# Linear attention on one core: K and V in 8 KB rows, V by DMA into zeroed blocks, the first matmul in 64x64 tiles

## The chip, the cores and the metric

The kernel runs on 1 core of one Trainium2 chip. The metric is device time of one execution, in microseconds. The time before is 126.32 us, the median of 3 runs (126.27 to 126.68).

## The reference

Inputs Q, K and V are float32 of shape (8, 12, 512, 64): 96 heads of 512 rows of 64 numbers. Each head is on its own.

```python
Q_feat = np.maximum(0, Q) + 1
K_feat = np.maximum(0, K) + 1
KV = np.einsum('bhkd,bhkv->bhdv', K_feat, V)
K_sum = np.sum(K_feat, axis=2)
numerator = np.einsum('bhqd,bhdv->bhqv', Q_feat, KV)
denominator = np.einsum('bhqd,bhd->bhq', Q_feat, K_sum)
return (numerator / (denominator[:, :, :, None] + 1e-10)).astype(np.float32)
```

So per head: a 64x64 matrix KV and a 64-vector K_sum from K and V, then for each row of Q a row of 64 numbers and its divisor. 12.6 MB come in three times, 12.6 MB go out.

## The kernel before, in words

Work goes in 12 groups of eight heads, and two groups make a round of sixteen heads (1 MB of bf16 for each of K, V and Q). All loads but the first half of Q are DMAs from POOL that cast float32 to bf16. SP loads that first half in float32 into an output buffer.

*Loads.* `load` (L115) brings K and V with 16 rows of a head in a partition: 4 KB read, 2 KB written in one run, 32 consecutive partitions to a head. `load_q` (L121) brings Q with 32 rows in a partition: 8 KB read, 4 KB written. After the first round, which is loaded in halves, a load of K, V or Q is one DMA of 128 partitions.

*First matmul.* `k_features` (L151, DVE) writes max(K + 1, 1) to a tile of its own. A partition holds rows of one head of four, so V must be spread out for the matmul: `v_blocks` (L167, L169) copies the 32 partitions of head b to columns 64b of `v_all`, zeros elsewhere (three copies on DVE, the fourth on ACT). `v_all` is zeroed once by `clear` (L254, L255), which also writes four columns of ones (L256). `keys_values` (L185) then does 16 x 2 matmuls per group, each with 128 rows of contraction, 64 columns of K and 260 of `v_all`: four heads' KV and their K_sum. The two of a pair go to the two halves of the columns of the array. ACT copies the results to `kva_all` (L195, L196), which is block-diagonal over two heads and cleared once by POOL (L276).

*Second matmul.* `q_features` (L151) and `transposes` (L206, with copies out of PSUM at L209, nearly all on ACT) bring Q into place. `out_matmuls` (L219) fills two PSUM tiles of two banks, `norms` does a reciprocal (L236) and a product (L237) for each of them on DVE and writes `o_sb`.

*Stores.* `store` puts the first ten of twelve groups out from POOL (L135), the last two from SP (L140 to L148), the last one in pieces. All stores are kept behind the loads in POOL's queue: four of them follow the last load, the others come one by one.

The order on every engine is the order of the program text (`tc.manual_schedule()`). A load waits until the tile's last reader is done (`IN_BUFS = 2`). `psum`, which the outputs use, has two tiles in all, so a chunk's matmuls wait for the norms of the chunk before it. DMAs from POOL use eight semaphores in turn, so one waits for the eighth before it to land.

Of the kernel before, what the change touches and what calls it, by code (L numbers as in the profile page):

```python
# [12 lines left out]
BANK = 512  # L13
IN_BUFS = 2
OUT_BUFS = 5
LAG = 3
# [3 lines left out]
def kernel(  # L20
# [15 lines left out]

# [5 lines left out]
    C2 = 2 * C  # L45
    C4 = 4 * C
    R = 4
    NPAIR = B * H * S // (P * C)
    NP = 4
    NG = NPAIR // NP  # L50
# [3 lines left out]
    def view(t, c):  # L54
        return t.flatten_outer_dims().rearrange("(n p c) d -> p n c d", p=P, c=c)

    q_eights = view(Q, C4)
    k_dram = view(K, C2)
    v_dram = view(V, C2)
    o_dram = view(out, C)  # L60
# [3 lines left out]
    kf_pool = ctx.enter_context(tc.tile_pool(name="kf_pool", bufs=2))  # L64
# [8 lines left out]
    identity = const.tile([P, P], BF16, name="identity")  # L73
    NV = 4
    v_all = const.tile([P, 2, 2, C2, 4 * D1], BF16, name="v_all")
    ones = const.tile([P, 4], BF16, name="ones")
    zero = const.tile([P, 1], FP32, name="zero")
    kva_all = const.tile([P, NV, 4, 2, D1], BF16, name="kva_all")
    kva_diag = [kva_all[:, i] for i in range(NV)]

    drams = dict(k=k_dram, v=v_dram)
    raw = {}
    bufs = {}
    kfs = {}
    qfs = {}
    qts = {}
    outs = {}
    cells_of = {}
# [7 lines left out]
    def load_rest_q(t):  # L96
        u = in_pool.tile([P, 2, C4, D], BF16, name="q_raw")
        nc.gpsimd.dma_start(out=u[:, 1], in_=q_eights[:, 1])
        for e in range(2):
            raw["q", e] = [  # L100
                x.rearrange("p (r c) d -> p r c d", c=C)[:, :, 4 * e : 4 * e + 4]
                for x in (t, u[:, 1])
            ]

    def load(x, groups):
        s = groups[0] // 2
        if groups[0] % 2 == 0 or (x, s) not in bufs:
            bufs[x, s] = in_pool.tile([P, 4, C2, D], BF16, name=f"{x}_raw")
        if len(groups) == 2:
            ms = slice(0, 4)  # L110
            of = slice(4 * s, 4 * s + 4)
        else:
            ms = slice(groups[0] % 2, 4, 2)
            of = slice(4 * s + groups[0] % 2, 4 * s + 4, 2)
        nc.gpsimd.dma_start(out=bufs[x, s][:, ms], in_=drams[x][:, of])  # L115
        for g in groups:
            raw[x, g] = bufs[x, s][:, g % 2 : 4 : 2]

    def load_q(s):
        t = in_pool.tile([P, 2, C4, D], BF16, name="q_raw")  # L120
        nc.gpsimd.dma_start(out=t, in_=q_eights[:, 2 * s : 2 * s + 2])  # L121
        rows = t.rearrange("p n (r c) d -> p n r c d", c=C)
        for e in range(2):
            raw["q", 2 * s + e] = [rows[:, n, :, 4 * e : 4 * e + 4] for n in range(2)]

    def load_pair(s):
        load("k", (2 * s, 2 * s + 1))
        load("v", (2 * s, 2 * s + 1))
        load_q(s)

    def store(g):
        s = g // 2
        o_to = o_dram[:, 2 * NP * s : 2 * NP * s + 2 * NP]
        if g < NG - 2:
            nc.gpsimd.dma_start(  # L135
                out=o_to[:, g % 2 : 2 * NP : 2], in_=outs[s][:, g % 2 : 2 * NP : 2], single_packet=True
            )
            return
        if g == NG - 2:
            nc.sync.dma_start(out=o_to[:, 0 : 2 * NP : 2], in_=outs[s][:, 0 : 2 * NP : 2])  # L140
            return
        o_sb = outs[s]
# [12 lines left out]
    def k_features(g):  # L155
        k_raw = raw.pop(("k", g))
        kf = kf_pool.tile([P, C2, 2, D], BF16, name="kf")
        for n in range(2):
            feature(kf[:, :, n], k_raw[:, n])
        kfs[g] = kf  # L160

    def v_blocks(g):
        v_raw = raw.pop(("v", g))
        for b in range(4):
            ps = slice(32 * b, 32 * b + 32)
            if b == 3:
                nc.scalar.copy(out=v_all[ps, g % 2, :, :, b * D : b * D + D], in_=v_raw[ps])  # L167
            else:
                nc.vector.tensor_copy(  # L169
                    out=v_all[ps, g % 2, :, :, b * D : b * D + D], in_=v_raw[ps]  # L170
                )

    def q_features(g):
        q_raw = raw.pop(("q", g))
        qf = qf_pool.tile([P, R, C // 2, 2, D], BF16, name="qf")
        for n in range(2):
            feature(qf[:, :, :, n], q_raw[n])
        qfs[g] = qf

    def keys_values(g):  # L180
        kf = kfs.pop(g)
        kva_ps = psum_kva.tile([P, 4 * D1], FP32, name="kva_ps")
        for c in range(C2):
            for n in range(2):
                nc.tensor.matmul(  # L185
                    kva_ps[64 * n : 64 * n + 64],
                    lhsT=kf[:, c, n, :],
                    rhs=v_all[:, g % 2, n, c, :],
                    start=(c == 0),
                    stop=(c == C2 - 1),  # L190
                )
        kva = kva_diag[g % NV]
        for n in range(2):
            ps = slice(64 * n, 64 * n + 64)
            nc.scalar.copy(out=kva[ps, :, n, 0:D], in_=kva_ps[ps, 0 : 4 * D].rearrange("p (b d) -> p b d", b=4))  # L195
            nc.scalar.copy(out=kva[ps, :, n, D], in_=kva_ps[ps, 4 * D : 4 * D1])  # L196

    def transposes(g):
        qf = qfs.pop(g)
        if g % 2 == 0:  # L200
            qts[g // 2] = mid_pool.tile([P, C, P, R], BF16, name="qt")
        for half in range(2):
            qt_ps = psum_qt.tile([P, 2, R, P], BF16, name="qt_ps")
            for c in range(2):
                for r in range(R):
                    nc.tensor.transpose(qt_ps[:, c, r], qf[:, r, 2 * half + c, :, :], identity)  # L206
            copy = nc.vector.tensor_copy if half and g == NG - 2 else nc.scalar.copy
            lo = g % 2 * 4 + 2 * half
            copy(out=qts[g // 2][:, lo : lo + 2], in_=qt_ps.rearrange("p c r q -> p c q r"))  # L209

    def out_matmuls(g, h):
        qt = qts[g // 2]
        kva = kva_diag[(g // 2 * 2 + h) % NV]
        ops = [psum.tile([P, 2, BANK], FP32, tag="ps", name="o_ps") for _ in range(2)]
        for c in range(C):
            for j in range(2):
                b = 2 * (g % 2) + j
                q = 16 * (4 * h + b)
# [3 lines left out]
                    rhs=kva[:, b],  # L222
# [3 lines left out]
        cells_of[g, h] = ops  # L226

    def norms(g, h):
        ops = cells_of.pop((g, h))
        if (g % 2, h) == (0, 0):  # L230
            outs[g // 2] = out_pool.tile([P, 2 * NP, C, D], FP32, name="o_sb")
        o_sb = outs[g // 2]
        for i in range(2):
# [4 lines left out]
                out=o_sb[:, 2 * h + g % 2 : 2 * NP : NP, 4 * i : 4 * i + 4].rearrange(  # L238
# [7 lines left out]
    def output(g):  # L246
        for h in range(2):
            out_matmuls(g, h)
            norms(g, h)

    def clear(i):
        t = v_all[:, i].rearrange("p n c x -> p (n c x)").bitcast(FP32)
        w = t.shape[1] * 5 // 8
        nc.vector.memset(t[:, 0:w], 0.0)  # L254
        nc.scalar.copy(out=t[:, w:], in_=zero.to_broadcast([P, t.shape[1] - w]))  # L255
        nc.vector.tensor_copy(  # L256
            out=v_all[:, i, :, :, 4 * D : 4 * D1].rearrange("p n c j -> p (n c) j"),
            in_=ones[:, None, :].to_broadcast([P, 2 * C2, 4]),
        )

    with tc.manual_schedule():
        nc.gpsimd.memset(zero, 0.0)
        q_first = load_first_q()
        load("k", (0,))
        load("v", (0,))
        load_rest_q(q_first)
        load("k", (1,))
        load("v", (1,))
        nc.vector.memset(ones, 0.0)
        for b in range(4):  # L270
            nc.vector.memset(ones[32 * b : 32 * b + 32, b : b + 1], 1.0)
        clear(0)
        make_identity(nc, identity)
        for t in kva_diag:
            for b in range(4):
                nc.gpsimd.memset(t[:, b], 0.0)  # L276
        load_pair(1)
        clear(1)
        last = NG - 1
        for g in range(last - 1):  # L280
            if g % 2:
                transposes(g - 1)
            k_features(g)
            v_blocks(g)
            if g >= 2:
                output(g - 2)
            if g % 2:
                transposes(g)
            else:
                q_features(g)  # L290
                q_features(g + 1)
            keys_values(g)
            if g % 2 and g // 2 + 2 < NG // 2:
                load_pair(g // 2 + 2)
            if g == NG - 5:
                for done in range(g - LAG):
                    store(done)
            if g >= NG - 5:
                store(g - LAG)
        k_features(last - 1)  # L300
        output(last - 3)
        out_matmuls(last - 2, 0)
        v_blocks(last - 1)
        k_features(last)
        v_blocks(last)
# [12 lines left out]
        for g in range(last - LAG, NG):  # L318
            store(g)
# [30 lines left out]
```

## Time and profile before

| | us |
|---|---|
| median of 3 runs | 126.32 |
| span of the profiled execution, first to last instruction | 124.5 |
| busy DVE | 89.7 |
| busy PE | 65.0 |
| busy ACT | 59.6 |
| busy POOL | 26.6 |

The page gives no other time of the profiled execution than its span; 1.8 us lie between the span and the median. Busy times are shares of the whole span and say nothing of who waits for whom. The rows "DMA" and "GB/s" cut the span in 40 slices of 3.1 us: 9 means that the 16 DMA engines were busy for 90% or more, and GB/s counts the bytes as written. "PEclk" is the clock granted to TensorE in tenths of full speed. A group's row has the busy time, the mean duration of one instruction, and the idle time before it with what ended it.

### The profile page before, as it was taken

How to read it: one execution, taken by the hardware profiler on the slowest of the kernel's cores; microseconds unless marked ns; L12 is line 12 of the kernel's file. 1: busy time of each engine (PE TensorE's matmuls, PEld its weight loads, DVE VectorE, ACT ScalarE, POOL GpSimd, SP SyncE). 2: the span in 40 equal slices, each digit the busy share in tenths (PEclk: the TensorE clock that was granted, in tenths of full speed). 3: DMA queues.
4: the chain of work that ended last, by engine and by line, in shares of the span. 5: the costliest groups of instructions: out<-in, count | busy, mean ns of one | idle time of the engine just before them, and what ended most of it. 6: DMA issues, size and time to landing. Idle time of an engine off the chain costs nothing.

```text
span 124.5 us, 2350 instructions
## 1 busy us (share of the span) xinstructions
PE 65.0 (52%) x960; PEld 53.1 (43%) x960; DVE 89.7 (72%) x190; ACT 59.6 (48%) x86; POOL 26.6 (21%) x53
## 2 busy tenths in 40 slices
PE   0000874600596837939197495987756987420000
PEld 0000754600475736829175374866635766210000
DVE  4875744206999989997999989999599996970000
ACT  7505069706009981398807767169990355000000
POOL 6992020400001310204002194202203302000000
PEclk9999999985559996799859959689985599955555
DMA  3999999999999999999999999999999999999993
GB/s 95 319 211 218 204 209 212 209 215 218 207 212 212 220 215 205 212 213 216 212 213 211 213 219 211 213 209 216 214 295 421 420 419 411 416 414 416 417 407 140
DMA packets 11971, 32.13 MB, mean 258 GB/s; under 512 B 568, under 2 KB 824, under 8 KB 11832
## 3 DMA queue, kind: packets, MB, share of 16 engines
q0 software_dynamic: 10592, 28.84, 97.5%
q1 hardware_dynamic: 1368, 3.15, 6.7%
q8 instruction: 7, 0.11, 0.3%
q14 instruction: 4, 0.03, 0.1%
HBM read 37.75 MB, written 12.58 MB: 404 GB/s over the span
## 4 chain that ended last, share of the span: by engine, by line
DMA 30%; DVE 27%; PE 14%; ACT 10%; POOL 6%; issue 3%; DVEq 0%; ACTq 0%; POOLq 0%
DMA v_raw<-in_V_dram 30%; DVE o_sb L237 12%; PE kva_ps L185 12%; DVE v_all L169 8%; ACT v_all L167 5%; ACT qt L209 3%; DVE recip L236 3%; DVE qf L151 2%; POOL kva_all L276 2%; POOL k_raw L115 2%; ACT kva_all L195 2%; PE qt_ps L206 1%; PE o_ps L219 1%; DVE kf L151 1%; POOL v_raw L115 1%
## 5 line engine op out<-in xcount | busy, mean ns | idle before, releaser
L185 PE MATMUL kva_ps<-v_all,kf 128*64 128x260 bf16 x384 | 34.2, 351 | 15.8 <-DVE v_all L169 14.2
L185 PEld LDWEIGHTS <-kf 128*64 128x64 bf16 x384 | 27.8, 144 | 19.7 <-DVE v_all L169 14.7
L237 DVE TENSOR_TENSOR o_sb<-o_ps,recip 128x512 f32<-128x512 f32 x48 | 33.2, 692 | 1.7
L219 PE MATMUL o_ps<-kva_all,qt 128*64 128x130 bf16 x384 | 19.6, 236 | 28.1 <-DVE recip L236 19.1
L169 DVE COPY v_all<-v_raw 32x2048 bf16<-32x2048 bf16 x36 | 25.5, 710 | 10.5 <-DMA v_raw<-in_V_dram 10.1
L219 PEld LDWEIGHTS <-qt 128*64 128x64 bf16 x384 | 13.7, 116 | 33.1 <-issue 16.9
L167 ACT COPY v_all<-v_raw 32x2048 bf16<-32x2048 bf16 x12 | 22.6, 1894 | 10.8 <-DMA v_raw<-in_V_dram 10.6
L195 ACT CAST kva_all<-kva_ps 64x256 bf16<-64x256 f32 x24 | 8.9, 370 | 31.4 <-PE kva_ps L185 31.2
L209 ACT COPY qt<-qt_ps 128x1024 bf16<-128x1024 bf16 x23 | 22.2, 1015 | 2.5 <-PE qt_ps L206 2.2
L206 PE MATMUL qt_ps<-identity,qf 128*128 128x128 bf16 x192 | 14.1, 229 | 1.3 <-ACT qt L209 1.1
L135 POOL DMA_DIRECT2D out_dram<-o_sb x10 | 8.8, 879 | 23.1 <-DMA q_raw<-in_Q_dram 6.7
L206 PEld LDWEIGHTS <-qf 128*128 128x128 bf16 x192 | 11.8, 103 | 4.1 <-issue 2.2
L115 POOL DMA_DIRECT2D k_raw<-in_K_dram x7 | 5.4, 772 | 37.5 <-DVE kf L151 37.0
L151 DVE TENSOR_SCALAR kf<-k_raw 128x1024 bf16<-128x1024 bf16 x24 | 9.9, 453 | 4.3 <-DMA k_raw<-in_K_dram 4.2
L236 DVE RECIPROCAL recip<-o_ps 128x8 f32<-128x8 f32 x48 | 9.6, 200 | 2.9 <-PE o_ps L219 2.6
L115 POOL DMA_DIRECT2D v_raw<-in_V_dram x7 | 5.4, 768 | 16.5 <-ACT v_all L167 16.5
L151 DVE TENSOR_SCALAR qf<-q_raw 128x1024 bf16<-128x1024 bf16 x22 | 8.1, 424 | 0.0
L254 DVE MEMSET v_all<- 128x2600 f32 x2 | 4.5, 2225 | 1.1 <-issue 1.1
L196 ACT CAST kva_all<-kva_ps 64x4 bf16<-64x4 f32 x24 | 4.1, 169 | 0.0
L121 POOL DMA_DIRECT2D q_raw<-in_Q_dram x5 | 3.5, 704 | 0.0
L255 ACT COPY v_all<-zero 128x1560 f32<-128x1560 f32 x2 | 2.9, 1488 | 0.0
L276 POOL MEMSET kva_all<- 128x130 bf16 x16 | 2.4, 196 | 0.0
(14 smaller groups left out, 6.6 us busy)
## 6 DMA issues: line engine op xcount, KB each, us to landing
out_dram<-o_sb POOLq DMA_DIRECT2D x10, 1024.0 KB, 24.0
k_raw<-in_K_dram POOLq DMA_DIRECT2D x5, 1024.0 KB, 16.7
v_raw<-in_V_dram POOLq DMA_DIRECT2D x5, 1024.0 KB, 17.3
q_raw<-in_Q_dram POOLq DMA_DIRECT2D x5, 1024.0 KB, 21.5
o_sb<-in_Q_dram SPq DMA_DIRECT2D x1, 1024.0 KB, 4.8
k_raw<-in_K_dram POOLq DMA_DIRECT2D x2, 512.0 KB, 9.5
v_raw<-in_V_dram POOLq DMA_DIRECT2D x2, 512.0 KB, 11.3
out_dram<-o_sb SPq DMA_DIRECT2D x1, 1024.0 KB, 12.1
```

The source lines that it names most:

```text
L115: nc.gpsimd.dma_start(out=bufs[x, s][:, ms], in_=drams[x][:, of])
L135: nc.gpsimd.dma_start(out=o_to[:, g % 2 : 2 * NP : 2], in_=outs[s][:, g % 2 : 2 * NP : 2], single_packet=True)
L151: nc.vector.tensor_scalar(out=dst, in0=src, scalar1=1.0, scalar2=1.0, op0=ALU.add, op1=ALU.max)
L167: nc.scalar.copy(out=v_all[ps, g % 2, :, :, b * D : b * D + D], in_=v_raw[ps])
L169: nc.vector.tensor_copy(out=v_all[ps, g % 2, :, :, b * D : b * D + D], in_=v_raw[ps])
L185: nc.tensor.matmul(kva_ps[64 * n : 64 * n + 64], lhsT=kf[:, c, n, :], rhs=v_all[:, g % 2, n, c, :], start=(c == 0), stop=(c == C2 - 1),)
L195: nc.scalar.copy(out=kva[ps, :, n, 0:D], in_=kva_ps[ps, 0 : 4 * D].rearrange("p (b d) -> p b d", b=4))
L206: nc.tensor.transpose(qt_ps[:, c, r], qf[:, r, 2 * half + c, :, :], identity)
L209: copy(out=qts[g // 2][:, lo : lo + 2], in_=qt_ps.rearrange("p c r q -> p c q r"))
L219: nc.tensor.matmul(ops[c // 4][64 * j : 64 * j + 64, c // 2 % 2, (c % 2) * W : (c % 2) * W + W], lhsT=qt[:, c, q : q + 16, :], rhs=kva[:, ...
L236: nc.vector.reciprocal(out=recip, in_=cells[:, :, :, :, D:D1])
L237: nc.vector.tensor_tensor(out=o_sb[:, 2 * h + g % 2 : 2 * NP : NP, 4 * i : 4 * i + 4].rearrange("p n (b c) d -> p b c n d", b=2), in0=cell ...
```

## The change

Sixteen heads are now one step, six in all. K and V are read with 32 rows of a head in a partition (8 KB read, 4 KB written), and heads are interleaved over the partitions: of each eight heads (the first eight are n = 0, the others n = 1), partition 4j + b holds rows of pair b, the first head of the pair in partitions 0 to 63 and the second in 64 to 127. Each load of K or V is four DMAs, one for each b, of 32 partitions with a step of 4.

V's DMAs write straight into `v_blocks`, nine blocks of 32 x 64 columns: block b for n = 0, b + 5 for n = 1, block 4 for the ones. It is zeroed once (`clear`) and never written elsewhere until the end, since partition 4j + b gets V in the blocks of b alone. The copies of V on DVE and ACT are gone. The ones come from a mask, a sum over the identity (`put_ones`).

K's features are written in place. `keys_values` does 32 x 4 matmuls per step, each with 64 rows of contraction (r), 64 columns of K (n) and 320 columns of `v_blocks`, to two PSUM tiles. It is cut in four parts, two of them ahead of the fourth chunk of outputs. `transposes` copies half of its results on DVE. The last two steps' outputs use the memory of `v_blocks` in place of an output buffer; there are four of those instead of five. The order of the main loop is new.

```diff
-OUT_BUFS = 5
-LAG = 3
+OUT_BUFS = 4
...
+    k_dram, v_dram = (
+        t.flatten_outer_dims().rearrange("(s n b j c) d -> s b j n c d", n=2, b=NB, j=J, c=C4)
+        for t in (K, V)
+    )
...
+    v_blocks = [const.tile([P, 2 * NB + 1, C4, D], BF16, name=f"v_blocks{i}") for i in range(2)]
...
+    def load_k(s):
+        k_raw[s] = in_pool.tile([P, 2, C4, D], BF16, name="k_raw")
+        for b in range(NB):
+            nc.gpsimd.dma_start(out=k_raw[s][b:P:NB], in_=k_dram[s, b])
+
+    def load_v(s):
+        for b in range(NB):
+            nc.gpsimd.dma_start(
+                out=v_blocks[s % 2][b:P:NB, b : b + NB + 2 : NB + 1], in_=v_dram[s, b]
+            )
...
-    def v_blocks(g):
-        v_raw = raw.pop(("v", g))
-        for b in range(4):
-            ps = slice(32 * b, 32 * b + 32)
-            if b == 3:
-                nc.scalar.copy(out=v_all[ps, g % 2, :, :, b * D : b * D + D], in_=v_raw[ps])
-            else:
-                nc.vector.tensor_copy(
-                    out=v_all[ps, g % 2, :, :, b * D : b * D + D], in_=v_raw[ps]
-                )
...
+    def k_features(s):
+        for n in range(2):
+            feature(k_raw[s][:, n], k_raw[s][:, n])
...
+    def keys_values(s, part):
+        if part == 0:
+            kva_ps[s] = [psum_kva.tile([P, BANK], FP32, name="kva_ps") for _ in range(2)]
+        kf = k_raw[s]
+        n_cols = (NB + 1) * D
+        for c in range(C4 // 4 * part, C4 // 4 * part + C4 // 4):
+            for n in range(2):
+                for r in range(2):
+                    ps = slice(64 * r, 64 * r + 64)
+                    nc.tensor.matmul(
+                        kva_ps[s][r][64 * n : 64 * n + 64, 0:n_cols],
+                        lhsT=kf[ps, n, c, :],
+                        rhs=v_blocks[s % 2][ps, NB * n : NB * n + NB + 1, c, :],
+                        start=(c == 0),
+                        stop=(c == C4 - 1),
+                    )
...
-            copy = nc.vector.tensor_copy if half and g == NG - 2 else nc.scalar.copy
+                copy = nc.vector.tensor_copy if half else nc.scalar.copy
...
+            if s < NS - 2:
+                outs[s] = out_pool.tile([P, 2 * NP, C, D], FP32, name="o_sb")
+            else:
+                t = v_blocks[s % 2].rearrange("p b c d -> p (b c d)").bitcast(FP32)
+                outs[s] = t[:, 0 : 2 * NP * C * D].rearrange("p (n c d) -> p n c d", n=2 * NP, c=C)
...
     def clear(i):
-        t = v_all[:, i].rearrange("p n c x -> p (n c x)").bitcast(FP32)
-        w = t.shape[1] * 5 // 8
+        t = v_blocks[i].rearrange("p b c d -> p (b c d)").bitcast(FP32)
+        w = t.shape[1] // 2
         nc.vector.memset(t[:, 0:w], 0.0)
         nc.scalar.copy(out=t[:, w:], in_=zero.to_broadcast([P, t.shape[1] - w]))
+
+    def put_ones(i):
         nc.vector.tensor_copy(
+            out=v_blocks[i][:, NB, :, 0:NB], in_=mask[:, None, :].to_broadcast([P, C4, NB])
         )
...
         q_first = load_first_q()
-        load("k", (0,))
-        load("v", (0,))
+        load_k(0)
         load_rest_q(q_first)
...
         clear(0)
+        load_v(0)
         make_identity(nc, identity)
...
+        load_k(1)
         clear(1)
...
+        load_v(1)
+        load_q(1)
...
+        for s in range(1, NS + 1):
+            if s + 1 < NS:
+                load_k(s + 1)
+                load_v(s + 1)
+                load_q(s + 1)
+            if s == NS - 2:
+                for g in range(2 * NS - 8):
+                    store(g)
+            if s < NS:
+                k_features(s)
+            for i in range(4):
+                out_matmuls(s - 1, *chunks[i])
+                if s < NS and i == 2:
+                    keys_values(s, 0)
+                    keys_values(s, 1)
+                norms(s - 1, *chunks[i])
+            if s < NS:
+                keys_values(s, 2)
+                keys_values(s, 3)
+                q_features(s)
+                keys_values_out(s)
+                transposes(s)
+            if s >= NS - 2:
+                for g in range(2 * s - 4, 2 * s - 2 if s < NS else 2 * NS):
+                    store(g)
```

## The prediction

> **What bounds the kernel now.** I read the page's slices first, then its queues, then the DMA issues.
>
> ```profile
> span 124.5 us, 2350 instructions
> ...
> DMA  3999999999999999999999999999999999999993
> GB/s 95 319 211 218 204 209 212 209 215 218 207 212 212 220 215 205 212 213 216 212 213 211 213 219 211 213 209 216 214 295 421 420 419 411 416 414 416 417 407 140
> ...
> q0 software_dynamic: 10592, 28.84, 97.5%
> q1 hardware_dynamic: 1368, 3.15, 6.7%
> q8 instruction: 7, 0.11, 0.3%
> ```
>
> The DMA row is full from the second slice to the last but one. Up to slice 30 the engines load at some 213 GB/s of bf16 written, which is 426 GB/s of float32 read; after that they store at 416 GB/s. So the span is one line of transfers: 37.75 MB in, 12.58 MB out, and what lies at its two ends. The chain of waits names DVE with 27%, but that chain runs beside a DMA that never rests, and POOL's long waits are for buffers, with transfers still queued:
>
> ```profile
> POOL k_raw L115 <- DVE kf L151: 37.0, 4, 14.0
> POOL v_raw L115 <- ACT v_all L167: 16.5, 4, 4.5
> ```
>
> The trace's records of single DMA packets give the rates (no view prints them). In them the first packet starts 1.8 us into the span and the last ends at 123.2. Each load ends with a tiny semaphore packet per engine. These lie 4.952 us apart for a whole load of K or V (32 packets per engine, 4 KB read each), 2.486 for a half (16 packets), 4.895 for a whole load of Q (16 packets, 8 KB read each) and 2.458 for a half (8 packets). Two equations each: a 4 KB packet takes 154.1 ns, an 8 KB one 304.6, and the end of a DMA 0.02 us (the semaphore packet itself is recorded with 22 ns).
>
> **The loads.** K and V go to 8 KB rows, Q's shape, but each load becomes four DMAs of 32 partitions. One quarter is 4 x 304.6 + 22 = 1240 ns per engine; four are 4.96 us against 4.952 now. The longer row saves 0.057 us per load and three more DMA ends take 0.066. Over twelve loads: +0.1 us at most, since the first K and V are two halves each today. If the ends cost nothing, the change would be -0.057 x 12 = -0.7 us. I take zero and keep -0.7 as the lower bound.
>
> The Trainium skill, DMA: Bandwidth & Descriptors, section Rules for kernel authors, asks for 128 partitions and at least 1 MiB per DMA, and calls splits over partitions useless; its fit gives every DMA about 2 us of fixed cost, by which 34 more DMAs that overlap nothing would add 68 us. The trace's halves, at 0.02 us more than half a whole, do not show such a cost where DMAs queue behind one another.
>
> **Does the queue stay fed?** Every POOL DMA now waits for the eighth before it to land (program order with its waits). Before, eight were up to 39 us of work; now at least seven quarters are left when one lands, 7 x 1.24 = 8.7 us. An issue takes 0.58 to 0.86 us on POOL (first loads in the timeline), and SP's first load took 1.0 us from issue to first packet, so 8.7 us covers it. POOL gets 34 more issues, at most 34 x 0.8 = 27 us, of 98 us that it is idle; behind them in its queue are Q's loads and the stores, which have the same cover.
>
> V's first load now waits for the zeroing. Rows:
>
> ```profile
> 1.87 2.23 DVE L254 MEMSET v_all<- 128x2600 f32 x1 [0.59 <-issue]
> 2.03 2.88 ACT L255 COPY v_all<-zero 128x1560 f32<-128x1560 f32 x2
> ```
>
> Per tile 9216 columns in two halves: DVE 4608 x 0.857 ns = 3.9 us, ACT 4608 x 0.92..0.95 = 4.4 us, from 2.03 to 6.4. Queued behind that wait on POOL are the identity, the clearing of kva_all (2.4 us today) and K's second load. Meanwhile DMA has the first Q (to 4.7 us), K (4.96) and the other Q half (2.46): to 12.2 us. V is issued from 6.4 to 9.5. Hidden, with some 4 us to spare; without that cover it would cost what it is late by.
>
> **The engines.** DVE loses the 36 copies of V (25.5 us), gains 11 copies of qt at 1.21 and 3.4 us of zeroing: some 81 us. ACT loses 22.6 us of V copies and 11 qt copies. None of this shortens a line that DMA sets. What counts is a round of sixteen heads (a load of K, V and Q, 14.8 us) and how long its chain is in the new order. TensorE rows:
>
> ```profile
> 33.57 3.67 PE L185 MATMUL kva_ps<-v_all,kf 128*64 128x260 bf16 x32
> ...
> 42.31 1.98 PE L185 MATMUL kva_ps<-v_all,kf 128*64 128x260 bf16 x32
> ```
>
> Two column tiles run together today: a pair of 260 columns starts every 110 ns at full clock, 215 at half. The new matmuls come in fours of 64x64 with 320 columns. No row here shows halves of the rows side by side. Bounds: all four together, 110 x 320/260 = 136 ns per four (4.4 us for the 32 of a round, 8.6 at half clock); two at a time, twice that. I take the first, since two tiles that share the moving data's partitions already run without loss. The Trainium skill, TensorEngine Tiling, section Tiling Modes, says that 64x64 tiles are four and independent, which gives the same 4.4 us; no run here shows it.
>
> One round is walked from the end of the last qt copy, at full clock. DVE does K features first, 1.3 us (an estimate; two of 1024 columns take 0.76). The outputs of the round before come in four chunks of two PSUM tiles, and a tile is free for the next chunk once its norms are done, 0.84 us each:
>
> ```profile
> 104.68 0.69 DVE L237 TENSOR_TENSOR o_sb<-o_ps,recip 128x512 f32<-128x512 f32 x1
> 105.28 0.20 DVE L236 RECIPROCAL recip<-o_ps 128x8 f32<-128x8 f32 x1
> 105.52 0.69 DVE L237 TENSOR_TENSOR o_sb<-o_ps,recip 128x512 f32<-128x512 f32 x1
> ```
>
> Three chunks of norms end at 6.3. TensorE has the third chunk out at 5.1, half of keys_values to 7.3, then the fourth chunk, whose norms end at 9.5; the second half ends at 10.2, Q features at 10.9. ACT first empties kva_ps (four pairs of 0.46), then copies qt; each qt_ps buffer waits for its copy, so the last copy, on DVE, ends at 15.5. At half clock throughout the same walk gives 21. TensorE's clock falls to half now and then today (the page's PEclk row; the mean from 52 to 66 us is 0.88), and in the norms' stretch it has little to do, so the first half of keys_values comes at half clock and the second mostly at full: I take 17. That is longer than 14.8: the arithmetic falls behind the loads by some 2 us per round, which buffers and stores absorb as follows. Round 1 ends at about 41 us (V of the first round lands at 18, keys_values and its copies to 26, one round from there). Four more rounds end at 109, the last eight norms at 116.5. The loads end at about 92.5; K's last load needs keys_values of round 3 (about 70) before 74. POOL's ten stores at 2.5 us then last to 117.5, and SP's two MB to 122.5. Its first store is ready at 113, the last piece is needed by about 120. So DMA never runs dry, and the end stays where it was. **Sum:** 124.5 + 0.0..0.1 of span; the page gives no other time for this execution, and the 1.8 us between span and the median of 126.32 are taken as unchanged. 126.4.
>
> **Rivals.**
> (a) The round is too long, the slower side. From L = 17.9 us per round the last norms pass 120 and each 0.1 more adds 0.4 us; at 19 the end is 41 + 4 x 19 + 7.3 + 1.6 = 126, 2.7 us late: 129. For it: my walk is only 0.9 below that point, and its clock is an estimate. Against: the granted clock was 0.88 in that stretch.
> (b) Row halves don't run together: 4.4 us more per round at full clock, 8.6 at half; L 20 to 25, loads wait for keys_values too: 136 to 145.
> (c) Instruction fetches. Page: q8 moved 7 packets; the records show 0.89 to 1.02 us each, and after each another single one of the 16 engines ends its later loads some 0.9 us behind. PE's matmuls and weight loads go from 1920 to 2688, so 10 fetches. On fresh engines that changes nothing; on one already late, or on one that gets the uneven last store piece (123 partitions of 512 B), the end moves by 0.6 to 0.9: 127.1.
> (d) Ends of DMAs overlap, or the tail evens out: -0.7, 125.6.
> (e) Every quarter waits for the one before it to land. Price from a row: the last semaphore packet of the first K at 7.82, DVE starting on it at 8.20, so 0.38 x 34 = 13: 139. Against: the halves. The fixed cost per DMA on the skill's DMA page is the rule that such an end would follow.
>
> **Chances.** Unchanged (126.0 to 126.7) 0.40; (a) 0.14; (b) 0.06; (c) 0.17; (d) 0.20; (e) 0.03. 0.3%, or 0.38 us, is about what a measurement of this kernel can tell from no change. Faster 0.20, same 0.40, slower 0.40. Range: from (d)'s 125.6 to 129.5, which leaves out (b), (e) and a small part of (a) and (d).
>
> **What would show it.** Right: DMA 9 throughout, K or V four quarters in 4.96 us, GB/s 213 then 416, DVE idle before kva and qt waits, the last norms near 116. Wrong: holes in the DMA row near 60 to 80 us (b), or after 112 (a); starts of four matmuls spread over 270 ns instead of 136 (b); a full DMA row but a longer last slice (c); quarter loads over 1.26 us (e) or under 1.23 (d).

## The result, and the profile after

The changed kernel takes 127.07 us (median of 20 runs, 126.85 to 127.74), the kernel before 126.31 (20 runs, 126.03 to 127.28). The ratio is 1.0053, with a 95% interval of 1.0034 to 1.0072: slower by 0.76 us, twice what a measurement of this kernel can tell from no change. The span of the profiled execution is 125.4 us against 124.5.

The page of the changed kernel, slices and queues (rows as in the prediction's first fence):

```profile
span 125.4 us, 3102 instructions
...
DMA  3999999999999999999999999999999999999991
GB/s 89 333 213 214 214 212 210 209 213 216 216 212 210 213 213 210 213 214 212 219 209 212 210 217 209 214 216 210 213 345 422 417 421 405 417 410 417 398 377 68
...
q0 software_dynamic: 8064, 28.84, 93.9%
q1 hardware_dynamic: 1368, 3.15, 6.8%
q8 instruction: 10, 0.16, 0.5%
```

The DMA row has no hole: loads at 213 GB/s, stores at about 416, as before. The bytes are the same, 28.84 and 3.15 MB. Two things differ. q8 fetched instructions 10 times in place of 7. And the end is ragged: 398, 377, 68 in the last three slices, where before had 417, 407, 140. Some DMA engines have finished while others still work. The end in stretches of 2 us, first after, then before (columns: stretch and its length, busy time of PE, PE's weight loads, DVE, ACT and POOL, the granted clock, DMA share, GB/s):

```profile
120.00:122.00 2.00, 0.00 (x0) 0.00 (x0) 0.00 (x0) 0.00 (x0) 0.00 (x0) 0.50 1.01 361
122.00:124.00 2.00, 0.00 (x0) 0.00 (x0) 0.00 (x0) 0.00 (x0) 0.00 (x0) 0.50 0.44 158
124.00:125.40 1.40, 0.00 (x0) 0.00 (x0) 0.00 (x0) 0.00 (x0) 0.00 (x0) 0.50 0.01 2
```

```profile
120.00:122.00 2.00, 0.00 (x0) 0.00 (x0) 0.00 (x0) 0.00 (x0) 0.00 (x0) 0.50 0.99 381
122.00:124.00 2.00, 0.00 (x0) 0.00 (x0) 0.00 (x0) 0.00 (x0) 0.00 (x0) 0.50 0.31 114
124.00:124.50 0.50, 0.00 (x0) 0.00 (x0) 0.00 (x0) 0.00 (x0) 0.00 (x0) 0.50 0.00 0
```

No compute engine has anything left to do after 120 us in either. In the records of single packets (which no view prints) the last packet ends at 124.16 after and 123.18 before. These 0.98 us make up the difference of the spans, since 1.3 us follow the last packet in both.

Which engines are late is read from the records too. Each store of POOL ends with a 4-byte packet per DMA engine, 16 in all; the records carry no engine number. For POOL's last store they lie, after, at 116.5 to 117.0 (seven), at 117.6 to 117.7 (seven), and at 119.03 and 119.16 (two). Two engines stand alone, 1.3 us behind the rest. Before, the sixteen lie between 118.5 and 121.6, and the last two are 0.3 apart. Two of 16 engines, behind by more than the time of one fetch (0.89 to 1.03 us in this trace), end the kernel.

### The profile page after: what moved, and what is told of

The parts are those of the page before. It is cut to its first block, busy times and chain, and to the rows that moved or that the text cites. A ratio compares the mean times of both kernels' runs of the same rounds, so it can differ in the third digit from the quotient of the medians.

```text
span 125.4 us, 3102 instructions
## 1 busy us (share of the span) xinstructions
PE 76.3 (61%) x1344; PEld 55.8 (45%) x1344; DVE 79.1 (63%) x149; ACT 32.0 (25%) x63; POOL 42.4 (34%) x75
## 3 DMA queue, kind: packets, MB, share of 16 engines
q0 software_dynamic: 8064, 28.84, 93.9%
q1 hardware_dynamic: 1368, 3.15, 6.8%
## 4 chain that ended last, share of the span: by engine, by line
PE 32%; DVE 23%; DMA 18%; ACT 14%; issue 7%; POOL 1%; DVEq 0%; ACTq 0%
PE kva_ps L154 24%; DMA q_raw<-in_Q_dram 10%; DVE o_sb L218 8%; DMA v_blocks<-in_V_dram 8%; DVE v_blocks L218 7%; PE o_ps L196 4%; DVE k_raw L130 4%; ACT kva_all L169 4%; PE qt_ps L183 4%; ACT qt L186 3%; ACT v_blocks L231 3%; DVE recip L217 3%; ACT kva_all L173 2%; POOL v_blocks L106 1%; ACT L231 1%
## 5 line engine op out<-in xcount | busy, mean ns | idle before, releaser
L154 PE MATMUL kva_ps<-v_blocks,k_raw 64*64 64x320 bf16 x768 | 35.9, 350 | 0.3 <-DMA v_blocks<-in_V_dram 0.3
L154 PEld LDWEIGHTS <-k_raw 64*64 64x64 bf16 x768 | 26.0, 127 | 8.1 <-issue 0.8
L186 DVE COPY qt<-qt_ps 128x1024 bf16<-128x1024 bf16 x12 | 14.7, 1225 | 14.3 <-PE qt_ps L183 13.8
L218 DVE TENSOR_TENSOR o_sb<-o_ps,recip 128x512 f32<-128x512 f32 x32 | 22.1, 692 | 1.1
L106 POOL DMA_DIRECT2D v_blocks<-in_V_dram x24 | 13.6, 570 | 26.0 <-DMA q_raw<-in_Q_dram 16.5
L102 POOL DMA_DIRECT2D k_raw<-in_K_dram x24 | 14.4, 607 | 14.7 <-PE kva_ps L154 12.0
L186 ACT COPY qt<-qt_ps 128x1024 bf16<-128x1024 bf16 x12 | 12.1, 1012 | 9.9 <-PE qt_ps L183 9.8
L218 DVE TENSOR_TENSOR v_blocks<-o_ps,recip 128x512 f32<-128x512 f32 x16 | 11.1, 692 | 0.6
L130 DVE TENSOR_SCALAR k_raw<-k_raw 128x2048 bf16<-128x2048 bf16 x12 | 8.0, 710 | 3.9 <-DMA k_raw<-in_K_dram 3.9
L231 ACT COPY v_blocks<-zero 128x4608 f32<-128x4608 f32 x2 | 8.0, 4029 | 0.0
```

The lines of the kernel that those rows point to most:

```text
L102: nc.gpsimd.dma_start(out=k_raw[s][b:P:NB], in_=k_dram[s, b])
L106: nc.gpsimd.dma_start(out=v_blocks[s % 2][b:P:NB, b : b + NB + 2 : NB + 1], in_=v_dram[s, b])
L130: nc.vector.tensor_scalar(out=dst, in0=src, scalar1=1.0, scalar2=1.0, op0=ALU.add, op1=ALU.max)
L154: nc.tensor.matmul(kva_ps[s][r][64 * n : 64 * n + 64, 0:n_cols], lhsT=kf[ps, n, c, :], rhs=v_blocks[s % 2][ps, NB * n : NB * n + NB + 1, c ...
L186: copy(out=qts[s][:, lo : lo + 2], in_=qt_ps.rearrange("p c r q -> p c q r"))
L218: nc.vector.tensor_tensor(out=o_sb[:, 2 * h + e : 2 * NP : NP, 4 * i : 4 * i + 4].rearrange("p n (b c) d -> p b c n d", b=2), in0=cells[:, ...
```

## The experiments

The runs come from three sessions, and each is compared with the kernel before of its own session: 126.34 us (23 runs), 126.18 (17 runs) or 126.28 (9 runs). Theory F is the prediction's case (c): instruction fetches make some engines late. The first rival, S: SP's last stores come out at 115.8 in place of 107.9, so their small packets are left alone at the end. The row of the kernel before:

```profile
107.92 0.39 SPq L140 DMA_DIRECT2D out_dram<-o_sb  x1
```

**1. Fewer instructions in the changed kernel (`fewer`).** Every second chunk of the first product is left out, and the matmuls that remain have 512 columns in place of 320.

```diff
-        n_cols = (NB + 1) * D
-        for c in range(C4 // 4 * part, C4 // 4 * part + C4 // 4):
+        n_cols = 2 * NB * D
+        for c in range(C4 // 4 * part, C4 // 4 * part + C4 // 4, 2):
...
-                        rhs=v_blocks[s % 2][ps, NB * n : NB * n + NB + 1, c, :],
+                        rhs=v_blocks[s % 2][ps, n : n + 2 * NB, c, :],
```

> The changed kernel with half of the first matmuls (every second c is left out, so half of the keys and values are not summed) and 512 columns in each of the others: TensorE streams 80% of the columns with 1922 instructions in place of 2690. Theory F (instruction fetches: ten of 16 KB, two of them on engines that had one before): seven fetches, no engine hit twice, the last packet 0.7 to 1.0 us earlier, 126.1 to 126.4. Theory S (SP's stores come 8 us later than before, so that DMA has small packets of one queue alone at the end): the round gets only some 1 us shorter, SP's first store at about 112, and the time stays within 0.3 us of 127.07.

Measured: 125.97 us (125.79 to 126.8, 12 runs), ratio 0.9969 (0.9947 to 0.9991). Page of this run:

```profile
span 124.0 us, 2334 instructions
...
GB/s 95 333 211 214 213 211 211 213 213 215 214 214 211 213 213 211 213 210 214 214 213 211 211 211 214 213 211 211 215 292 419 419 421 417 412 419 411 417 406 158
...
q8 instruction: 7, 0.11, 0.3%
```

Seven fetches, the last slices are even again (417, 406, 158), and 1.10 us of the changed kernel's time are gone. But rounds got shorter as well (SP's first store at 111.4 in place of 115.8), so run 5 had to separate the two.

**2. More instructions in the kernel before (`before_more`).**

```diff
+        for c in range(C2):
+            for n in range(2):
+                nc.tensor.matmul(
+                    kva_ps[64 * n : 64 * n + 64, 4 * D1 + c : 4 * D1 + c + 1],
+                    lhsT=kf[:, c, n, :],
+                    rhs=v_all[:, g % 2, n, c, 0:1],
+                    start=True,
+                    stop=True,
+                )
```

> The kernel before with 384 more matmuls of one column after each group's keys_values (32 per group, into PSUM columns that nobody reads): TensorE has 2690 instructions like the changed kernel. Theory F: ten fetches in place of seven, engines hit twice, 0.6 to 1.0 us slower: 126.9 to 127.3. Theory S: stores from SP at most 2 us later than before, so 126.3 to 126.5.

Measured: 127.5 us (127.22 to 127.97, 8 runs), ratio 1.0079 (1.005 to 1.0108). Nothing of the change is in this kernel; it has the old loads, the old copies of V and the old order. With 2688 instructions of PE, as many as the changed kernel has (the expectations say 2690), it shows the same signs:

```profile
span 126.2 us, 3118 instructions
...
GB/s 112 290 200 214 206 206 206 212 212 221 204 213 212 217 217 206 211 213 220 208 212 210 219 214 208 212 212 217 215 336 418 421 414 414 409 413 415 414 370 54
...
q8 instruction: 10, 0.16, 0.5%
```

**3. and 4. Doses between (`before_more8`, `before_more9`).** The added matmuls with `range(6)` and `range(11)` in place of `range(C2)`, 2208 and 2448 instructions of PE.

> The kernel before with 288 more PE instructions (one-column matmuls, 6 a group in place of the 16 that made 127.5): 2210, so 8 fetches of 16 KB. F (the fetches go round eight DMA engines, and only the ninth lands on one that is already late): no change, 126.3 to 126.5. Rival D (every added instruction or fetch costs its share: 6/16 of the 1.16 us that 768 instructions cost, or 1/3 of it for one fetch more): 126.7 to 126.8.

> The kernel before with 528 more PE instructions (11 one-column matmuls a group): 2450, so 9 fetches. F: the ninth lands on an engine that is late already, and the end moves by nearly the whole step, 127.1 to 127.5. Rival D (a share for each instruction, 11/16, or for each fetch, 2/3): 127.1 as well at most; what tells the two apart is the run with 8 beside this one (F: 0 and then +0.9; D: +0.4 and +0.8).

Measured: 126.27 us (126.08 to 127.55, 11 runs), ratio 1.0021 (1.0 to 1.0041), and 127.14 us (126.95 to 128.36, 6 runs), ratio 1.0097 (1.0067 to 1.0127). Rows of the first, then of the second:

```profile
span 124.5 us, 2638 instructions
...
q8 instruction: 8, 0.13, 0.4%
```

```profile
span 125.5 us, 2878 instructions
...
q8 instruction: 9, 0.15, 0.4%
```

The cost is a step, not a slope. 288 instructions and one fetch more cost 0.09 us, within what can't be told from nothing; the next 240, with the ninth fetch, cost 0.87. Rival D, a share for each instruction or fetch, asked for 126.7 at eight fetches. Nine of the eleven runs lie at 126.4 or below, but the interval of the ratio just reaches 126.7, so the times alone make D unlikely and don't exclude it. The landings, read below the table, decide.

**5. The instructions put back, but not the work (`fewer_more`).** Kernel 1, with each left-out chunk done as matmuls of one column.

```diff
+            for n in range(2):
+                for r in range(2):
+                    ps = slice(64 * r, 64 * r + 64)
+                    nc.tensor.matmul(
+                        kva_ps[s][r][64 * n : 64 * n + 64, 0:1],
+                        lhsT=kf[ps, n, c + 1, :],
+                        rhs=v_blocks[s % 2][ps, n, c + 1, 0:1],
+                        start=False,
+                        stop=(c == C4 - 2),
+                    )
```

> The run that left out every second chunk of the first product (125.97), with the left-out chunks put back as one-column matmuls: the instructions are 2690 again (10 fetches), while PE's time in the first product stays about half of the changed kernel's. It computes the first product only in part. F: 10 fetches bring the time back to 126.9 to 127.2. Rival R (the changed kernel is late because its rounds of 17 us put SP's stores at 115.8; fewer instructions helped only through shorter rounds): SP's first store stays near 111 to 112, and the time at 125.9 to 126.1.

Measured: 127.07 us (126.86 to 127.45, 6 runs), ratio 1.0072 (1.006 to 1.0085).

```profile
span 125.7 us, 3102 instructions
...
GB/s 94 322 205 214 214 210 215 210 209 216 215 210 215 210 215 213 210 216 211 212 213 214 214 211 213 215 211 210 218 340 422 417 411 417 411 418 416 407 376 50
...
q8 instruction: 10, 0.16, 0.5%
```

The time is back, with the ragged end (407, 376, 50). SP's first store came 2.5 us earlier than in the changed kernel, with no gain from it:

```profile
113.28 0.40 SPq L120 DMA_DIRECT2D out_dram<-v_blocks  x1
```

Rival R is refuted: the length of the rounds was not the cause. SP's store also came a little later than I had said (113.3, not 111 to 112): the one-column matmuls are not free for PE.

The kernels so far and those below fall into one table. "Apart" counts the engines whose last landing of POOL's last store comes 1.2 us or more after the fourteen or fifteen others.

| kernel | fetches | engines apart | change against before |
|---|---|---|---|
| before | 7 | 0 | |
| `fewer` | 7 | 0 | -0.37 |
| `before_more8` | 8 | 0 | +0.09 |
| `before_more9` | 9 | 1 | +0.96 |
| `before_more` | 10 | 2 | +1.16 |
| `fewer_more` | 10 | 2 | +0.89 |
| after | 10 | 2 | +0.76 |

In all of them, and in the four runs below (10 fetches, two engines apart in each), the engines apart number the fetches beyond eight. The reading that fits: the fetches go round eight engines, each hit costs its engine about one fetch, and the ninth and tenth fall on engines that have lost that time already.

That the same engine is hit twice can be read from the landings, though no engine has a number there. From one store of POOL to the next the sixteen nearly keep their distances; the engine that a fetch has held up changes its place. In `before_more9`, after eight fetches, the landings of the store that begins to land at 103.92 form two groups: eight lie within 0.57 us of the first one, and eight come 1.07 to 1.58 us after it. Between this store and the next lies the ninth fetch, at 107.21. In the next store the early group still has eight members and the late one seven: the landing at 1.41 is gone, and one stands at 2.51. In the changed kernel the fetches at 103.38 and 109.30 do the same, each taking one engine out of the late group (1.36 to 2.51, 1.39 to 2.51). The durations of the fetches point to a turn of eight as well: they run through 0.974, 0.961, 0.893, 0.893, 0.948, 0.945, 0.936 and 0.974 us in the changed kernel, through the same to 0.001 us in `fewer_more`, and in `tail119` through the same cycle begun two places earlier.

**6. SP's stores early (`spread`).** One quarter of the first product after each chunk of outputs, in place of halves after the third and the fourth.

```diff
-                if s < NS and i == 2:
-                    keys_values(s, 0)
-                    keys_values(s, 1)
+                if s < NS:
+                    keys_values(s, i)
                 norms(s - 1, *chunks[i])
             if s < NS:
-                keys_values(s, 2)
-                keys_values(s, 3)
```

> The changed kernel with one quarter of keys_values after each chunk of outputs, in place of two after the third and two at the end; nothing is left out and the instructions are the same in number. DVE no longer waits 4 us per round for TensorE, the round falls from 17 us to about 14.8, where the loads set it, and SP's first store comes at about 105 in place of 115.8. Theory S: the time goes back to 126.3. Theory F: still ten fetches, the engines hit twice still end last: 126.8 to 127.1.

Measured: 129.46 us (129.34 to 130.68, 6 runs), ratio 1.0257 (1.0219 to 1.0294). Page and a window of this run, and SP's first store in its timeline:

```profile
span 127.8 us, 3107 instructions
...
GB/s 100 324 214 210 212 214 209 213 214 214 212 212 214 212 214 212 213 210 219 210 210 214 213 213 213 212 213 214 254 406 424 410 418 413 419 417 415 412 128 0
```

```profile
104.08 0.40 SPq L120 DMA_DIRECT2D out_dram<-v_blocks  x1
```

```profile
122.00:124.00 2.00, 0.00 (x0) 0.00 (x0) 0.00 (x0) 0.00 (x0) 0.00 (x0) 0.50 0.28 107
124.00:127.80 3.80, 0.00 (x0) 0.00 (x0) 0.00 (x0) 0.00 (x0) 0.00 (x0) 0.50 0.00 0
```

SP's stores came 11.7 us earlier, the transfers ended at 123.93, 0.2 us earlier than in the changed kernel, and yet the time rose by 2.4 us. S is refuted, and F didn't foresee this either. The window shows what it is: nothing moves in the last 3.8 us. In the records a closing DRAIN instruction on POOL ends at 127.0, 3.1 us after the last landing of a POOL store (123.92), and the other engines wait for it. In the changed kernel the same instruction ends 3.1 us after POOL's last store too (119.16, 122.24), but behind it SP's stores still run to 124.16, so it is covered. Here POOL's store was the last transfer of all.

**7. and 8. POOL's stores moved to SP (`spread_sp`, `spread_sp7`).** Kernel 6 with the ninth and tenth store, then the sixth to tenth, issued by SP in place of POOL (the condition of the second is `g < 2 * NS - 7`; with the last two, SP then has seven of the twelve):

```diff
-        if g < 2 * NS - 2:
+        if g < 2 * NS - 4:
...
-        if g == 2 * NS - 2:
-            nc.sync.dma_start(out=o_to[:, 0 : 2 * NP : 2], in_=o_sb[:, 0 : 2 * NP : 2])
+        if g < 2 * NS - 1:
+            nc.sync.dma_start(out=o_to[:, g % 2 : 2 * NP : 2], in_=o_sb[:, g % 2 : 2 * NP : 2])
```

> The run with a quarter of the first product after each chunk (129.46), with its two last stores of POOL issued by SP, so that POOL's closing drain starts after the loads and not after the last store. Theory P (POOL's drain runs on for about 3 us behind POOL's last store, and the span ends with it when that store is the last transfer): 2.3 to 2.6 us less, 126.9 to 127.2, since the 10 fetches remain. Rival Q (the early stores of SP themselves cost it, by small packets between POOL's): 128.9 to 129.5 still.

> The same spread of the first product, with seven of the twelve stores on SP (the fifth to eleventh of POOL's move there), so that POOL's share of 5 MB is through well before SP's 7 MB. In the run with two stores moved POOL's last store still landed last (123.3 us of a span of 127.0), so it did not take the drain off the end. Theory P (the span ends some 3.9 us after the last transfer when POOL's store is the last, 1.3 us when SP's is): SP's transfers end last, at 123.5 to 124.2 with 10 fetches, and the time is 126.5 to 127.2. Rival Q (SP's early stores cost it, whoever ends last): 128.5 or more.

Measured: 128.66 us (128.16 to 128.76, 4 runs), ratio 1.0192 (1.0175 to 1.021), and 128.11 us (127.93 to 128.22, 5 runs), ratio 1.0137 (1.0114 to 1.0159). Both numbers missed P's range, and Q's as well. In the first, POOL's last store landed at 123.27, and SP's last packet came 0.7 us after it, at 123.97, so the text on record for `spread_sp7` is wrong to call POOL's store the last to land. But POOL's DRAIN ended at 126.20 and still closed the kernel: the span ended 3.0 us after the last packet. In the second the drain was off the end, at 123.0, with the last packet at 124.96 and the span's end 1.5 us behind that:

```profile
span 126.4 us, 3107 instructions
...
GB/s 93 328 211 219 211 207 210 218 215 207 211 218 215 207 213 216 213 209 213 218 213 211 228 248 254 253 249 258 251 247 253 367 414 408 417 417 417 405 376 40
```

So the tail between last packet and end went from 3.86 us to 1.5, which is P's mechanism. But SP's stores, mixed with the loads from the 23rd slice on (228 to 258 GB/s), put the last packet 0.8 us later than in the changed kernel. Why SP's share ends so late wasn't settled.

**9. Another cut of the last store (`tail119`).** The last tile's store as 119 and 9 partitions, whole, in place of the three pieces.

```diff
-        cut = C - 2
-        for ps in (slice(0, 123), slice(123, P)):
-            nc.sync.dma_start(out=o_to[ps, 7, cut:], in_=o_sb[ps, 7, cut:])
-        nc.sync.dma_start(out=o_to[:, 7, 0:cut], in_=o_sb[:, 7, 0:cut])
+        for ps in (slice(0, 119), slice(119, P)):
+            nc.sync.dma_start(out=o_to[ps, 7], in_=o_sb[ps, 7])
```

> The changed kernel with the last tile's store (256 KB) as 119 and 9 partitions of 2 KB, in place of 192 KB over all engines and 64 KB on three. If a store of 119 partitions runs on the seven lowest engines (17 packets each, 1.4 us), the others lose their eight packets of 1536 B (0.49 us). Theory F: the two engines hit twice end last, so the end comes 0.5 us earlier, 126.6, if they are not among those seven, and up to 0.9 us later if they are. Theory S: the last data come at the same time, no gain, or a loss of up to 0.9 us.

Measured: 127.68 us (126.73 to 129.44, 12 runs), ratio 1.0088 (1.0056 to 1.012). The profiled run was the fastest, 126.73. Its transfers end at 123.57, 0.6 us earlier than in the changed kernel; the other runs lie up to 128.4, but for one. A likely reason is that the engines hit twice and those with the larger piece coincide in some runs and not in others, as the turn of the fetches begins at another place in this trace than in the changed kernel's; since the other runs have no trace, this stays open.

## What held of the prediction, and what did not

The forecast was 126.4, no change; the time is 127.07. It lies inside the range, but the likeliest case was the wrong one: rival (c), at a chance of 0.17, is what happened. That its 127.1 fits so well is in part luck. Ten fetches against seven cost 1.1 to 1.3 us in the runs (`before_more` against before 1.16, `fewer_more` against `fewer` 1.26, the changed kernel against `fewer` 1.13, each by its change against before), more than the 0.6 to 0.9 of (c), and the rest of the change, as far as `fewer` shows it, gave back 0.37, which the sum doesn't have.

**The loads: right.** A quarter takes 1.239 us per engine by its semaphore packets, 1.240 predicted. The last loads land at 91.2 to 92.7, before at 91.2 to 93.0. The ends of DMAs neither overlap nor cost more than their 0.02 us, so rivals (d), as far as it is about the loads, and (e) fall. The Trainium skill has a fixed cost of about 2 us for each DMA (DMA: Bandwidth & Descriptors, Anatomy of one DMA); if nothing hid it, the 34 DMAs more would cost an estimated 68 us by it. The trace shows 0.02 us each where DMAs queue behind one another.

**V's zeroing hidden, the queue fed: right.** The DMA row is full from the second slice on, and the first quarter of V lands 1.24 us after the other half of Q, so nothing waited for the zeroing.

**The four tiles: right.** At full clock a four of 64x64 with 320 columns starts every 136 ns (records of PE), as predicted. The Trainium skill, TensorEngine Tiling (Array Packing), Tiling Modes, has the four tiles independent; this trace agrees. The round of keys_values at s = 5, in the timeline of PE:

```profile
99.50 4.48 PE L154 MATMUL kva_ps<-v_blocks,k_raw 64*64 64x320 bf16 x64
...
104.74 2.37 PE L154 MATMUL kva_ps<-v_blocks,k_raw 64*64 64x320 bf16 x64
```

The same 64 matmuls take 4.48 us at half clock and 2.37 at full clock (granted 0.50 and 1.00 in these stretches). The clock's place was predicted, the first half slow, the second fast: in the five rounds the first half takes 3.47 to 4.48 us, the second 2.37 each time.

**The round: right.** keys_values begin at 29.6, 47.6, 64.5, 81.4 and 99.5, so 17 to 18 us apart, 17 predicted. It is then TensorE that DVE waits for, as the waits show:

```profile
DVE recip L217 <- PE o_ps L196: 17.1, 6, 4.0
DVE qt L186 <- PE qt_ps L183: 13.8, 11, 2.4
```

The last norms came later than I said, at 118.5 to 119.2 and not 116.5, and SP's first store at 115.8, not 113; 17.9 us per round was my tipping point, and this was nearer to it than the sum had it. It cost next to nothing: `fewer_more` had SP's stores out 2.5 us sooner and took the same 127.07 us, and in `spread`, with 11.7 us, the transfers ended only 0.2 us sooner.

```profile
115.83 0.40 SPq L120 DMA_DIRECT2D out_dram<-v_blocks  x1
...
118.47 0.69 DVE L218 TENSOR_TENSOR v_blocks<-o_ps,recip 128x512 f32<-128x512 f32 x1
```

**The end "stays where it was": wrong.** This is the step that failed. The term for instruction fetches was zero in the sum, on the ground that fetches fall on fresh engines. It should have been about +1.1: the fetches after the eighth put engines a second fetch behind, and the end moves with the first of them, by 0.87 us at the ninth. In the changed kernel the last packet moved from 123.18 to 124.16. The count, 10, and the time of one, 0.9 us, were right. The trace of before had seven fetches on seven different engines, which fits a turn of sixteen as well as one of eight; the forecast took the kinder of the two for its likeliest case, though nothing in the trace preferred it. With even odds between them (c) would have stood beside the forecast as an equal.

What is left over: with seven fetches the changed kernel's structure (`fewer`) stands 0.37 us below the kernel before. That is the gain of sign (d) that the sum left at zero. It leaves out half of the first product, so it isn't shown that the full kernel would have it without the fetches.

## What to carry to other kernels

Where DMA is busy from end to end, count TensorE's instructions too: in these traces each 256 of them cost one fetch of 16 KB that delays a single DMA engine by 0.9 us, which costs nothing measurable until an engine is hit that is late already. Halving the tiles of a matmul doubled its instructions here, so a change that frees DVE and ACT can pay for it on the DMA engines. Read the last slices of the GB/s row: here an uneven end with full rows before it came from single engines that were late.

## What the runs showed of the hardware that was not expected

- The fetches come with the count of PE's instructions, about every 256 matmuls and weight loads: in the eleven traces the k-th one starts when PE has issued 256 k, give or take 100, whenever that is. Eight of them cost nothing measurable (+0.09 us), the ninth 0.87 us more, and the engine that it held up was one that an earlier fetch had made late.
- POOL's closing DRAIN ends 2.9 to 3.1 us after the last landing of its stores in the changed kernel and its six variants, and 1.7 us in the kernel before and its three. The first issue 59 to 64 DMAs from POOL, the others 30; whether that or the order of the program makes the difference, no run here separates. When POOL's store is the last transfer, the span ends 3.9 us after the last packet (`spread`) instead of 1.3. In these kernels the last transfer is better SP's than POOL's.
